# Matrix-memory heads and attention value products on full 128-row tiles, in a streaming encoder step

## The chip, the cores and the metric

The kernel runs on one core of a Trainium2 chip. The metric is device time in microseconds (us) of one execution. Beside the plain runs there is one profiled execution, from which all rows of the trace come. Engines are called as in the profile: PE is TensorE (PEld its weight loads), DVE VectorE, ACT ScalarE, POOL GpSimd, SP SyncE.

## The reference

One layer of a hybrid encoder works on 256 prompt tokens and 64 sample tokens, each with 2048 features, all in float32:

```python
z = x @ w_in                                   # 2048 x 7184
attn  = chunk_band_attention(qa, ka, va)       # 16 heads x 64, chunks of 64 queries, softmax with position bias
h_b   = mlstm(conv_silu(qk), vb, ib, fb)       # 8 heads x 128, matrix memory C, normaliser n, stabiliser m
mix   = concat(head_rms(attn), head_rms(h_b) * sigmoid(ob)) @ w_out
x1    = layer_norm(ALPHA * x + mix)
y     = layer_norm(ALPHA * x1 + (silu(x1 @ w_gate) * (x1 @ w_up)) @ w_down)   # 2048 x 5632
```

The two mixers matter here. For one matrix-memory head and one run of tokens:

```python
s   = (q @ k.T) * exp(d - m_t)                          # causal, d from the gates
num = s @ v + w_inter * (q @ C);  den = s.sum + w_inter * (q @ n)
h   = num / max(|den|, exp(-m_t))
C_new = w_old * C + (w_k * k).T @ v                     # and n_new alike
```

The prompt's 256 tokens start with an empty state, the sample's 64 tokens with a given one. In attention each chunk of 64 queries attends to the keys of up to eight chunks before it and its own, which for the sample are 512 cached keys and 64 new ones.

## The kernel before

**Projections.** All 320 tokens (256 + 64) are kept as columns; a weight matrix is cut into pieces of 128 x 1024 numbers. For every piece SP starts a load (`load_piece`, L95), ACT rounds it to a high half `hi` (L124), DVE makes the low half `lo` by subtraction (L125), and PE does three matmuls for each of the piece's eight 128 x 128 weight tiles (L174, L175, L177), 128 x 320 each: 24 matmuls per piece. `run_plan` (L151) goes through the plan of pieces. Loads run up to three pieces ahead, the split into halves two (`LOOKAHEAD`).

**What hangs on them.** When the last piece of a strip of 256 weight columns is done, the strip's function is called, and it may start generators. `advance` (L134) gives each active generator one step behind every piece, so that the steps of the mixers stand on PE between the matmuls of two pieces; a bare `yield` lets one piece go by. The strips of the input projection come in four units u, each an attention part (`A(u)`, four heads in two pairs i) and a matrix-memory part (`M(u)`, two heads); the four strips of the output gate follow. The tile framework places the instructions on the engines' queues and adds the waits; inside `tc.manual_schedule` the written order stands.

**Attention, `attn_gen` (L341).** One run per pair of heads, eight in all. It transposes values and keys to token rows (L352, L353; `vtok` holds three blocks of tokens, the third with 64 rows) and cached keys (L358), makes scores (L374 to L379), adds the bias (L386), takes exponentials (L391), transposes them into `pT` (L399, L402, and L405 for the blocks of 64 keys, which fill rows 0 to 63), and multiplies them with the values (L419): 11 terms for two heads. The weights of a value product are 64 columns of `pT`, so the two heads s = 0, 1 stand in the two column halves of the array. Seven of the 11 terms have 128 keys as array rows, four have 64.

**Matrix memory, `mlstm_gen` (L577).** One run per head, eight in all. It transposes the values (L588), weights them by the gates (L593), makes the decay matrix `E` (L595 to L597, masked on POOL by L599), the scores (L603 for the first prompt block, L604 the second, L605 the sample's 64 tokens), multiplies scores and decay (L608), transposes the keys (L614), and copies them out (L616, L617). Two pieces later eight matmuls follow in a fixed order (L624 to L631): numerators of the prompt (L624 to L626) and of the sample (L627), the sample's product with the old state (L628), and the new states (L629 to L631). Norms follow on DVE and ACT, and after three more pieces the transposes of the result (L671). Every tile of the sample has 64 token rows or columns: L605, L627, L628, L631 and the third transposes of L614, L588 and L671.

Each fp32 matmul of the mixers stands in the trace as two matmul records with a weight load each; a transpose and a matmul of the projections stand as one.

**Other things that the change touches.** `init_static` (L285) clears `qbd`, `obd` and sets the column of ones of `vt1`, on POOL. `attn_loads` (L293) starts, from POOL, the loads of cached keys and values and of the bias rows `tz` of a unit. The convolution's result `y` (L565) and `E` (L594) are tiles of rotating pools with two buffers.

Of the kernel before, what the change touches and what calls it, by code (L numbers as in the profile page):

```python
# [13 lines left out]
ALU = mybir.AluOpType  # L14
# [46 lines left out]
def _build(tc, nc, I, O, es):  # L61
# [216 lines left out]
            mixbuf[nm] = big.tile([P, 8, T], F32R, tag="Bb", bufs=2, name="mix_" + nm)  # L278


    qbd = [const.tile([P, 5, P], F32, name="qbd%d" % i) for i in range(2)]
    obd = [const.tile([P, 5, P], F32, name="obd%d" % i) for i in range(2)]
    vt1 = [const.tile([P, 3, 129], F32, name="vt%d" % i) for i in range(2)]

    def init_static():  # L285
        for t in qbd + obd:
            G.memset(t, 0.0)
        for t in vt1:
            G.memset(t[:, :, 128:129], 1.0)

    attn = {}

    def attn_loads(u):  # L293
        a = {}
        u1 = big.tile([P, 8 * T], F32, tag="Bb", bufs=2, name="u1")
# [7 lines left out]
        G.dma_start(out=a["ck"], in_=I["cache_attn_k"][:, cs].rearrange("(n p) c -> p n c", p=P))  # L303
        G.dma_start(out=a["cv"], in_=I["cache_attn_v"][:, cs].rearrange("(n p) c -> p n c", p=P))
        a["tz"] = []
        for i in range(2):
            tz = mx.tile([P, BAND], F32, tag="tz", bufs=2, name="tz")
            for s in range(2):
                h = u * 4 + i * 2 + s
                src = bass.AP(tensor=fdram.tensor, offset=fdram.offset + h * 640,  # L310
                              ap=[[1, 64], [1, BAND]])
                G.dma_start(out=tz[s * 64:(s + 1) * 64, :], in_=src)
            a["tz"].append(tz)
        a["ktok"] = mx.tile([P, 3, 256], F32, tag="ktok", bufs=1, name="ktok")
        a["vtok"] = mx.tile([P, 3, 256], F32, tag="vtok", bufs=1, name="vtok")
        a["kT"] = [None, None]
        a["vT"] = [None, None]
        attn[u] = a
# [22 lines left out]
    def attn_gen(u, i):  # L341
# [62 lines left out]
        for j, s0 in enumerate((512, 1088, 1152)):  # L404
# [2 lines left out]
        yield  # L407
        yield
        ox = w_tile()
        terms = {0: [(10, 64, vtok, 0)], 1: [(4, P, vtok, 0)],  # L410
                 2: [(7, P, vtok, 0), (9, 64, vtok, 1)], 3: [(5, P, vtok, 0), (6, P, vtok, 1)],
                 4: [(j, P, cv, j) for j in range(4)] + [(8, 64, vtok, 2)]}
        with tc.manual_schedule(engines={PE}):
            for c in range(5):
                for m, (j, n, src, k) in enumerate(terms[c]):
                    for s in range(2):
                        r = slice(s * 64, (s + 1) * 64)
                        v0 = i * P + s * 64
                        TE.matmul(ox[r, c * 64:(c + 1) * 64], pT[0:n, j, r], src[0:n, k, v0:v0 + 64],  # L419
                                  start=(m == 0), stop=(m == len(terms[c]) - 1))  # L420
        rs = mx.tile([P, 5], F32, tag="rs", bufs=2, name="rs")
        V.reciprocal(rs, sm)
# [50 lines left out]
    def gates_done(ps):  # L473
# [19 lines left out]
        st = mx.tile([P, T], F32, tag="oth", bufs=2, name="gst")  # L493
        G.memset(st, 0.0)
        g = st[0:8, :]
# [11 lines left out]
        V.tensor_scalar(st[32:40, :], wk, KSC, None, ALU.mult)  # L507
# [4 lines left out]
        V.tensor_copy(st[64:72, :], e1)  # L512
# [14 lines left out]
    def gates_gen(st):  # L527
        for _ in range(5):
            yield
        ps = w_tile()  # L530
        for i, (t0, n) in enumerate(TOK):
            TE.transpose(ps[0:n, i * P:(i + 1) * P], st[:, t0:t0 + n], ident)
        gc = const.tile([P, 3, P], F32, name="gcol")
        V.tensor_copy(gc[:, 0:2, :], ps[:, 0:256].rearrange("p (n c) -> p n c", c=P))
        V.tensor_copy(gc[0:SS, 2, :], ps[0:SS, 256:384])
# [11 lines left out]
    def qk_done(u, kind, ps):  # L547
        for i in range(2):
# [28 lines left out]
    def mlstm_gen(h, i):  # L577
# [11 lines left out]
        V.tensor_copy(vt[:, 0:2, 0:P], ps[:, 0:256].rearrange("p (n c) -> p n c", c=P))  # L589
        V.tensor_copy(vt[0:SS, 2, 0:P], ps[0:SS, 256:384])  # L590
        wkv = mx.tile([P, 3, 129], F32, tag="wkv", bufs=2, name="wkv")
        for j, (t0, n) in enumerate(TOK):
            V.tensor_scalar(wkv[0:n, j, :], vt[0:n, j, :], gc[0:n, j, 32 + h:33 + h], None, ALU.mult)  # L593
# [8 lines left out]
        ps = w_tile()  # L602
        TE.matmul(ps[:, 0:256], k[:, 0:128], q[:, 0:256], start=True, stop=True)  # L603
        TE.matmul(ps[:, 256:384], k[:, 128:256], q[:, 128:256], start=True, stop=True)  # L604
        TE.matmul(ps[0:SS, 384:448], k[:, QS0:CO], q[:, QS0:CO], start=True, stop=True)  # L605
        sT = E
        for n, c0, c1 in ((P, 0, 384), (SS, 384, 448)):
            V.scalar_tensor_tensor(out=sT[0:n, c0:c1], in0=ps[0:n, c0:c1],  # L608
                                   scalar=0.25 * 128.0 ** -0.5, in1=E[0:n, c0:c1],
                                   op0=ALU.mult, op1=ALU.mult)  # L610
        pk = w_tile()
        for j, (t0, n) in enumerate(TOK):
            t1 = QS0 if j == 2 else t0
            TE.transpose(pk[0:n, j * P:(j + 1) * P], k[:, t1:t1 + n], ident)  # L614
        kt = mx.tile([P, 3, P], F32, tag="mkt", bufs=2, name="mkt")
        S.copy(kt[:, 0:2, :], pk[:, 0:256].rearrange("p (n c) -> p n c", c=P))  # L616
        S.copy(kt[0:SS, 2, :], pk[0:SS, 256:384])  # L617
        yield
        yield
        pn = w_tile()  # L620
        pc = w_tile()
        n0, n1, n2 = pn[:, 0:129], pn[:, 129:258], pn[0:SS, 258:387]
        with tc.manual_schedule(engines={PE}):
            TE.matmul(n0, sT[:, 0:128], vt[:, 0, :], start=True, stop=True)  # L624
            TE.matmul(n1, sT[:, 128:256], vt[:, 0, :], start=True, stop=False)
            TE.matmul(n1, sT[:, 256:384], vt[:, 1, :], start=False, stop=True)  # L626
            TE.matmul(n2, sT[0:SS, 384:448], vt[0:SS, 2, :], start=True, stop=True)  # L627
            TE.matmul(pc[0:SS, 0:129], q[:, QS0:CO], cn, start=True, stop=True)  # L628
            TE.matmul(pc[:, 129:258], kt[:, 0, :], wkv[:, 0, :], start=True, stop=False)  # L629
            TE.matmul(pc[:, 129:258], kt[:, 1, :], wkv[:, 1, :], start=False, stop=True)  # L630
            TE.matmul(pc[:, 258:387], kt[0:SS, 2, :], wkv[0:SS, 2, :], start=True, stop=True)  # L631
        nd = mx.tile([P, 3, 129], F32, tag="nd", bufs=2, name="nd")
        V.tensor_copy(nd[:, 0:2, :], pn[:, 0:258].rearrange("p (n c) -> p n c", c=129))
        it = mx.tile([SS, 129], F32, tag="it", bufs=1, name="it")
        S.mul(it, pc[0:SS, 0:129], gc[0:SS, 2, 96 + h:97 + h])
        V.tensor_tensor(out=nd[0:SS, 2, :], in0=n2, in1=it, op=ALU.add)
# [30 lines left out]
        yield  # L667
        yield
        ph = w_tile()
        for j, (t0, n) in enumerate(TOK):  # L670
            TE.transpose(ph[:, t0:t0 + n], hn[0:n, j, :], ident[0:n, 0:n])  # L671
# [401 lines left out]
```

## Time and profile before

| | us |
|---|---|
| three runs | 1601.16, 1604.15, 1606.2 (median 1604.15) |
| the profiled execution | 1601.19 |
| its span, first to last instruction | 1599.2 |
| DVE busy | 836.4 (52%) |
| ACT busy | 631.9 (40%) |
| POOL busy | 122.9 (8%) |
| DMA, queue of SP | 220.23 MB, 45.2% of the 16 engines' span |

The busy time of PE is that of pipelined matmuls whose ends are modelled: a matmul of the projections shows 0.31 us, but the next one starts 0.15 us behind it. What a matmul costs is therefore read from start to start. In rows of the timeline the first column is the start of a group of like instructions that follow each other, the second its duration from the first start to the last end, then engine, line, operation, output and inputs, rows * columns of the array for PE, the moving operand, and the count. The input projection with the mixers takes the first 520 us or so, the output projection stands up to about 640 us, and the feed-forward network makes up the rest.

### The profile page before, as it was taken

What the parts mean: (1) busy time and instruction counts of PE and PEld (TensorE: products, weight loads), DVE (VectorE), ACT (ScalarE), POOL (GpSimd) and SP (SyncE); (2) the same over time, 40 slices, a digit from 0 to 9 for tenths busy, and PEclk for the clock granted to TensorE, in tenths of its full rate; (3) what the DMA queues carried; (4) which work ended last, traced back from release to release, by engine and by line L of the source; (5) the groups of instructions that cost most, each with busy time, mean ns of one, the idle gap of its engine ahead of it and who ended that gap; (6) DMA issues with size and microseconds to landing.
All of it is one profiled execution on the core that took longest, in us unless ns stands there. A gap on an engine that the chain in (4) does not pass through costs nothing.

```text
span 1599.2 us, 26591 instructions
## 1 busy us (share of the span) xinstructions
PE 1577.6 (99%) x10906; PEld 1547.5 (97%) x10906; DVE 836.4 (52%) x1512; ACT 631.9 (40%) x972; POOL 122.9 (8%) x254
## 2 busy tenths in 40 slices
PE   8999999999999999999999999999999999999997
PEld 6999999999999999899999999999999999999996
DVE  4486575665765755944334444444434434443456
ACT  4455444444444533643333233333333333323332
POOL 4013101101100100400000000000000000000004
PEclk9999999999999999999999999999999999999997
DMA  9546454554444544355444454444454444444442
GB/s 322 173 144 175 146 147 128 149 146 130 122 126 137 172 143 145 106 164 153 145 153 151 146 153 150 147 153 149 146 157 145 148 155 146 151 153 145 152 138 66
DMA packets 225545, 238.99 MB, mean 149 GB/s; under 512 B 8683, under 2 KB 219819, under 8 KB 225227
## 3 DMA queue, kind: packets, MB, share of 16 engines
q1 hardware_dynamic: 220384, 220.23, 45.2%
q0 software_dynamic: 5040, 17.07, 3.2%
q8 instruction: 85, 1.39, 0.4%
q14 instruction: 36, 0.29, 0.1%
HBM read 230.85 MB, written 10.07 MB: 151 GB/s over the span
## 4 chain that ended last, share of the span: by engine, by line
PE 95%; DVE 2%; DMA 1%; issue 0%; SPq 0%; ACT 0%; DVEq 0%; ACTq 0%
PE mm L174 30%; PE mm L177 30%; PE mm L175 29%; PE w L419 1%; DMA raw<-w_in 1%; PE w L771 1%; DVE lo L125 1%; DMA xq<-x_sample 1%; PE w L375 0%; PE w L399 0%; PE w L614 0%; DVE ytp L1035 0%; PE w L352 0%; PE w L402 0%; PE w L358 0%; PE w L377 0%
## 5 line engine op out<-in xcount | busy, mean ns | idle before, releaser
L125 DVE TENSOR_TENSOR lo<-raw,hi 128x1024 fp32r<-128x1024 f32 (+1 forms) x409 | 501.0, 1225 | 599.1 <-ACT hi L124 599.0
L124 ACT CAST hi<-raw 128x1024 fp32r<-128x1024 f32 (+1 forms) x409 | 428.1, 1047 | 746.2 <-PE mm L175 641.3
L177 PE MATMUL mm<-x1h,lo 128*128 128x320 f32 (+1 forms) x1408 | 436.5, 310 | 2.2 <-DVE lo L125 2.2
L174 PE MATMUL mm<-x1l,hi 128*128 128x320 f32 (+1 forms) x1408 | 435.5, 309 | 0.9 <-DVE np L844 0.9
L175 PE MATMUL mm<-x1h,hi 128*128 128x320 f32 (+1 forms) x1408 | 435.6, 309 | 0.0
L174 PE MATMUL mm<-xlo,hi 128*128 128x320 f32 x912 | 288.4, 316 | 0.2 <-ACT hi L124 0.2
L175 PE MATMUL mm<-xhi,hi 128*128 128x320 f32 x912 | 281.3, 309 | 0.0
L177 PE MATMUL mm<-xhi,lo 128*128 128x320 f32 x896 | 277.6, 310 | 0.5 <-DVE lo L125 0.5
L177 PEld LDWEIGHTS mm<-x1h,lo 128*128 128x128 f32 x1408 | 265.8, 189 | 2.7 <-DVE lo L125 2.7
L174 PEld LDWEIGHTS mm<-x1l,hi 128*128 128x128 f32 x1408 | 265.4, 188 | 1.4 <-DVE np L844 1.3
L175 PEld LDWEIGHTS mm<-x1h,hi 128*128 128x128 f32 x1408 | 265.4, 188 | 0.0
L174 PE MATMUL mm<-hl,hi 128*128 128x320 f32 x704 | 218.0, 310 | 0.0
L177 PE MATMUL mm<-hh,lo 128*128 128x320 f32 x704 | 217.5, 309 | 0.0
L175 PE MATMUL mm<-hh,hi 128*128 128x320 f32 x704 | 217.5, 309 | 0.0
L174 PEld LDWEIGHTS mm<-xlo,hi 128*128 128x128 f32 x912 | 171.8, 188 | 2.5 <-ACT hi L124 0.4
L175 PEld LDWEIGHTS mm<-xhi,hi 128*128 128x128 f32 x912 | 172.0, 189 | 0.0
L177 PEld LDWEIGHTS mm<-xhi,lo 128*128 128x128 f32 x896 | 168.8, 188 | 1.0 <-DVE lo L125 1.0
L175 PEld LDWEIGHTS mm<-hh,hi 128*128 128x128 f32 x704 | 132.2, 188 | 0.0
L174 PEld LDWEIGHTS mm<-hl,hi 128*128 128x128 f32 x704 | 132.2, 188 | 0.0
L177 PEld LDWEIGHTS mm<-hh,lo 128*128 128x128 f32 x704 | 132.2, 188 | 0.0
L779 POOL TENSOR_TENSOR ytp<-ytp,g 128x256 f32<-128x256 f32 x16 | 13.6, 874 | 894.6 <-ACT ytp L776 894.6
L888 DVE SCALAR_TENSOR_TENSOR y<-y,mm 128x320 f32<-128x320 f32 x96 | 46.5, 484 | 49.0 <-PE mm L177 48.6
(313 smaller groups left out, 1343.2 us busy)
## 6 DMA issues: line engine op xcount, KB each, us to landing
raw<-w_in SPq DMA_DIRECT2D x114, 512.0 KB, 3.7
raw<-w_ffn_gate SPq DMA_DIRECT2D x88, 512.0 KB, 3.5
raw<-w_ffn_up SPq DMA_DIRECT2D x88, 512.0 KB, 3.5
raw<-w_ffn_down SPq DMA_DIRECT2D x88, 512.0 KB, 3.5
raw<-w_out SPq DMA_DIRECT2D x32, 512.0 KB, 3.5
tz<-fdram POOLq DMA_DIRECT2D x16, 144.0 KB, 2.9
xq<-x_prompt SPq DMA_DIRECT2D x4, 512.0 KB, 9.1
u<-cache_attn_k POOLq DMA_DIRECT2D x4, 512.0 KB, 6.0
```

The costliest lines, as they stand in the source:

```text
L124: S.copy(hi[:, cs], raw[:, cs])
L125: V.tensor_tensor(out=lo[:, cs], in0=raw[:, cs], in1=hi[:, cs].bitcast(F32), op=ALU.subtract)
L174: TE.matmul(o, hi[:, sl], xl, start=st, stop=False)
L175: TE.matmul(o, hi[:, sl], xh, start=False, stop=en and pc.perm)
L177: TE.matmul(o, lo[:, sl], xh, start=False, stop=en)
L419: TE.matmul(ox[r, c * 64:(c + 1) * 64], pT[0:n, j, r], src[0:n, k, v0:v0 + 64], start=(m == 0), stop=(m == len(terms[c]) - 1))
L771: TE.transpose(dst[j][:, i * P:(i + 1) * P], y[:, 2 * s + i, t0:t0 + n], ident)
L779: G.tensor_tensor(out=keep[0][:, j, cs], in0=keep[0][:, j, cs], in1=late["g2"][:, cs], op=ALU.mult)
L888: V.scalar_tensor_tensor(out=y[:, c, :], in0=y[:, c, :], scalar=ALPHA if g == 0 else 1.0, in1=ps[i][:, 0:T], op0=ALU.mult, op1=ALU.add)
```

## The change

All matmuls and transposes on the sample's 64 tokens, and the value products with 64 keys, are issued with 128 rows and (outside of the value products, whose weights stay 64 columns wide) 128 weight columns. The tiles that they read get the missing rows or columns, and these are set to zero.

- `vtok`, `E` and the convolution's results become tiles that are made once (`vtok`, `Es`, `cys`), with 128 tokens' worth of space in the sample's block; `init_static` clears the space on POOL. `qbd`, `obd`, `vt1` move to the pool of the mixers.
- `attn_loads` clears rows 64 to 127 of the three 64-key blocks of `pT`, for every unit, on POOL.
- L605's weights become 128 columns of k (64 of them zero); the moving operand stays 64 columns.
- L627, L628, L631 and the transposes L532, L614, L671 take full tiles. For L627 the weights are columns 384 to 511 of `E`, for L628 128 columns of q.
- Some pairs of instructions that treated prompt and sample apart become one: the products with the decay (L608), the copies of the transposed keys (L616, L617) and of the gates (L534, L535). `wkv`, `it` and the sum of L636 are made on 128 rows.

```diff
     def init_static():
         for t in qbd + obd:
             G.memset(t, 0.0)
         for t in vt1:
+            G.memset(t[64:128, 2, :], 0.0)
             G.memset(t[:, :, 128:129], 1.0)
+        G.memset(vtok[64:128, 2, :], 0.0)
+        for i in range(2):
+            for k in "qk":
+                G.memset(cys[k][i][:, CO:CO + SS], 0.0)
+            G.memset(Es[i][:, 384:512], 0.0)
...
+    vtok = mx.tile([P, 3, 256], F32, name="vtok")
+    Es = [mx.tile([P, 512], F32, name="E%d" % i) for i in range(2)]
+    cys = {k: [mx.tile([P, CO + SS], F32, name="cy%s%d" % (k, i)) for i in range(2)] for k in "qk"}
...
-        a["vtok"] = mx.tile([P, 3, 256], F32, tag="vtok", bufs=1, name="vtok")
+        a["vtok"] = vtok
+        G.memset(a["pT"][64:128, 8:11, :], 0.0)
...
-                        TE.matmul(ox[r, c * 64:(c + 1) * 64], pT[0:n, j, r], src[0:n, k, v0:v0 + 64],
+                        TE.matmul(ox[r, c * 64:(c + 1) * 64], pT[:, j, r], src[:, k, v0:v0 + 64],
                                   start=(m == 0), stop=(m == len(terms[c]) - 1))
...
-        E = mx.tile([P, 448], F32, tag="E", bufs=2, name="E")
+        E = Es[i]
...
-        TE.matmul(ps[0:SS, 384:448], k[:, QS0:CO], q[:, QS0:CO], start=True, stop=True)
+        TE.matmul(ps[:, 384:448], k[:, QS0:QS0 + P], q[:, QS0:CO], start=True, stop=True)
         sT = E
-        for n, c0, c1 in ((P, 0, 384), (SS, 384, 448)):
-            V.scalar_tensor_tensor(out=sT[0:n, c0:c1], in0=ps[0:n, c0:c1],
-                                   scalar=0.25 * 128.0 ** -0.5, in1=E[0:n, c0:c1],
-                                   op0=ALU.mult, op1=ALU.mult)
+        V.scalar_tensor_tensor(out=sT[:, 0:448], in0=ps[:, 0:448], scalar=0.25 * 128.0 ** -0.5,
+                               in1=E[:, 0:448], op0=ALU.mult, op1=ALU.mult)
         pk = w_tile()
-        for j, (t0, n) in enumerate(TOK):
-            t1 = QS0 if j == 2 else t0
-            TE.transpose(pk[0:n, j * P:(j + 1) * P], k[:, t1:t1 + n], ident)
+        for j, t1 in enumerate((0, P, QS0)):
+            TE.transpose(pk[:, j * P:(j + 1) * P], k[:, t1:t1 + P], ident)
...
-            TE.matmul(n2, sT[0:SS, 384:448], vt[0:SS, 2, :], start=True, stop=True)
-            TE.matmul(pc[0:SS, 0:129], q[:, QS0:CO], cn, start=True, stop=True)
+            TE.matmul(n2, sT[:, 384:512], vt[:, 2, :], start=True, stop=True)
+            TE.matmul(pc[:, 0:129], q[:, QS0:QS0 + P], cn, start=True, stop=True)
...
-            TE.matmul(pc[:, 258:387], kt[0:SS, 2, :], wkv[0:SS, 2, :], start=True, stop=True)
+            TE.matmul(pc[:, 258:387], kt[:, 2, :], wkv[:, 2, :], start=True, stop=True)
...
-        for j, (t0, n) in enumerate(TOK):
-            TE.transpose(ph[:, t0:t0 + n], hn[0:n, j, :], ident[0:n, 0:n])
+        for j in range(3):
+            TE.transpose(ph[:, j * P:(j + 1) * P], hn[:, j, :], ident)
```

More of the change, by code (lines that the diff above doesn't have):

```diff
@@ L278, in mix_tiles_b @@
             mixbuf[nm] = big.tile([P, 8, T], F32R, tag="Bb", bufs=2, name="mix_" + nm)
-    qbd = [const.tile([P, 5, P], F32, name="qbd%d" % i) for i in range(2)]
-    obd = [const.tile([P, 5, P], F32, name="obd%d" % i) for i in range(2)]
-    vt1 = [const.tile([P, 3, 129], F32, name="vt%d" % i) for i in range(2)]
+    qbd = [mx.tile([P, 5, P], F32, name="qbd%d" % i) for i in range(2)]
+    obd = [mx.tile([P, 5, P], F32, name="obd%d" % i) for i in range(2)]
+    vt1 = [mx.tile([P, 3, 129], F32, name="vt%d" % i) for i in range(2)]
     def init_static():
@@ L409, in attn_gen @@
         ox = w_tile()
-        terms = {0: [(10, 64, vtok, 0)], 1: [(4, P, vtok, 0)],
-                 2: [(7, P, vtok, 0), (9, 64, vtok, 1)], 3: [(5, P, vtok, 0), (6, P, vtok, 1)],
-                 4: [(j, P, cv, j) for j in range(4)] + [(8, 64, vtok, 2)]}
+        terms = {0: [(10, vtok, 0)], 1: [(4, vtok, 0)],
+                 2: [(7, vtok, 0), (9, vtok, 1)], 3: [(5, vtok, 0), (6, vtok, 1)],
+                 4: [(j, cv, j) for j in range(4)] + [(8, vtok, 2)]}
         with tc.manual_schedule(engines={PE}):
             for c in range(5):
-                for m, (j, n, src, k) in enumerate(terms[c]):
+                for m, (j, src, k) in enumerate(terms[c]):
                     for s in range(2):
@@ L492, in gates_done @@
                                  op0=ALU.mult, op1=ALU.add)
-        st = mx.tile([P, T], F32, tag="oth", bufs=2, name="gst")
+        st = mx.tile([P, 3 * P], F32, tag="oth", bufs=2, name="gst")
         G.memset(st, 0.0)
-        g = st[0:8, :]
+        g = st[0:8, 0:T]
         V.tensor_tensor(out=g, in0=ig, in1=F, op=ALU.subtract)
@@ L506, in gates_done @@
             S.activation(wk[:, a:b], g[:, a:b], AF.Exp, bias=nM[:, b - 1:b])
-        V.tensor_scalar(st[32:40, :], wk, KSC, None, ALU.mult)
+        V.tensor_scalar(st[32:40, 0:T], wk, KSC, None, ALU.mult)
         e1 = t8("e1")
@@ L511, in gates_done @@
         S.activation(e1, e1, AF.Exp)
-        V.tensor_copy(st[64:72, :], e1)
+        V.tensor_copy(st[64:72, 0:T], e1)
         wi = mx.tile([HB, SS], F32, tag="g8_wi", name="wi")
@@ L530, in gates_gen @@
         ps = w_tile()
-        for i, (t0, n) in enumerate(TOK):
-            TE.transpose(ps[0:n, i * P:(i + 1) * P], st[:, t0:t0 + n], ident)
+        for i in range(3):
+            TE.transpose(ps[:, i * P:(i + 1) * P], st[:, i * P:(i + 1) * P], ident)
         gc = const.tile([P, 3, P], F32, name="gcol")
-        V.tensor_copy(gc[:, 0:2, :], ps[:, 0:256].rearrange("p (n c) -> p n c", c=P))
-        V.tensor_copy(gc[0:SS, 2, :], ps[0:SS, 256:384])
+        V.tensor_copy(gc, ps[:, 0:384].rearrange("p (n c) -> p n c", c=P))
         gate["col"] = gc
@@ L563, in qk_done @@
             S.activation(th, acc, AF.Tanh, scale=0.5)
-            y = mx.tile([P, CO], F32, tag="conv" + kind, bufs=2, name="cy")
-            V.scalar_tensor_tensor(out=y, in0=th, scalar=1.0, in1=acc, op0=ALU.add, op1=ALU.mult)
+            y = cys[kind][i]
+            V.scalar_tensor_tensor(out=y[:, 0:CO], in0=th, scalar=1.0, in1=acc, op0=ALU.add, op1=ALU.mult)
             ml[(kind, 2 * u + i)] = y
@@ L591, in mlstm_gen @@
         wkv = mx.tile([P, 3, 129], F32, tag="wkv", bufs=2, name="wkv")
-        for j, (t0, n) in enumerate(TOK):
-            V.tensor_scalar(wkv[0:n, j, :], vt[0:n, j, :], gc[0:n, j, 32 + h:33 + h], None, ALU.mult)
-        E = mx.tile([P, 448], F32, tag="E", bufs=2, name="E")
+        for j in range(3):
+            V.tensor_scalar(wkv[:, j, :], vt[:, j, :], gc[:, j, 32 + h:33 + h], None, ALU.mult)
+        E = Es[i]
         S.activation(E[:, 0:256], nM[:, 0:256], AF.Exp, bias=gc[:, 0, h:h + 1])
@@ L621, in mlstm_gen @@
         pc = w_tile()
-        n0, n1, n2 = pn[:, 0:129], pn[:, 129:258], pn[0:SS, 258:387]
+        n0, n1, n2 = pn[:, 0:129], pn[:, 129:258], pn[:, 258:387]
         with tc.manual_schedule(engines={PE}):
@@ L626, in mlstm_gen @@
             TE.matmul(n1, sT[:, 256:384], vt[:, 1, :], start=False, stop=True)
-            TE.matmul(n2, sT[0:SS, 384:448], vt[0:SS, 2, :], start=True, stop=True)
-            TE.matmul(pc[0:SS, 0:129], q[:, QS0:CO], cn, start=True, stop=True)
+            TE.matmul(n2, sT[:, 384:512], vt[:, 2, :], start=True, stop=True)
+            TE.matmul(pc[:, 0:129], q[:, QS0:QS0 + P], cn, start=True, stop=True)
             TE.matmul(pc[:, 129:258], kt[:, 0, :], wkv[:, 0, :], start=True, stop=False)
             TE.matmul(pc[:, 129:258], kt[:, 1, :], wkv[:, 1, :], start=False, stop=True)
-            TE.matmul(pc[:, 258:387], kt[0:SS, 2, :], wkv[0:SS, 2, :], start=True, stop=True)
+            TE.matmul(pc[:, 258:387], kt[:, 2, :], wkv[:, 2, :], start=True, stop=True)
         nd = mx.tile([P, 3, 129], F32, tag="nd", bufs=2, name="nd")
         V.tensor_copy(nd[:, 0:2, :], pn[:, 0:258].rearrange("p (n c) -> p n c", c=129))
-        it = mx.tile([SS, 129], F32, tag="it", bufs=1, name="it")
-        S.mul(it, pc[0:SS, 0:129], gc[0:SS, 2, 96 + h:97 + h])
-        V.tensor_tensor(out=nd[0:SS, 2, :], in0=n2, in1=it, op=ALU.add)
+        it = mx.tile([P, 129], F32, tag="it", bufs=1, name="it")
+        S.mul(it, pc[:, 0:129], gc[:, 2, 96 + h:97 + h])
+        V.tensor_tensor(out=nd[:, 2, :], in0=n2, in1=it, op=ALU.add)
         cw = mx.tile([P, 2, 129], F32, tag="cw", bufs=2, name="cw")
@@ L669, in mlstm_gen @@
         ph = w_tile()
-        for j, (t0, n) in enumerate(TOK):
-            TE.transpose(ph[:, t0:t0 + n], hn[0:n, j, :], ident[0:n, 0:n])
+        for j in range(3):
+            TE.transpose(ph[:, j * P:(j + 1) * P], hn[:, j, :], ident)
         ht = mx.tile([P, T], F32, tag="hst", bufs=8, name="hst")
@@ L682, in ob_done @@
                 advance()
-            th = mx.tile([P, T], F32, tag="oth", bufs=2, name="oth")
+            th = mx.tile([P, 3 * P], F32, tag="oth", bufs=2, name="oth")[:, 0:T]
             S.activation(th, ps[i][:, 0:T], AF.Tanh, scale=0.5)
```

3 lines of the change are left out of this document (1 added, 2 removed).

## The prediction

> **What bounds the kernel now.** I read the page first, then the waits of PE, the busy time by stretches, and last the timeline of PE around each edited line.
>
> ```profile
> PE 1577.6 (99%) x10906; PEld 1547.5 (97%) x10906; DVE 836.4 (52%) x1512; ACT 631.9 (40%) x972; POOL 122.9 (8%) x254
> ```
>
> ```profile
> PE 95%; DVE 2%; DMA 1%; issue 0%; SPq 0%; ACT 0%; DVEq 0%; ACTq 0%
> ```
>
> The first row is the busy time, the second the chain that ended last: 95% of it is PE. The edited lines all run between 80 and 490 us, so the question is whether PE waits for anything there. The waits of PE from 40 to 520 us have one row:
>
> ```profile
> PE mm L177 <- DVE lo L125: 0.5, 1, 0.5
> ```
>
> One wait of 0.5 us for DVE in 480 us. A busy PE is not a PE at its peak, though, and here that matters: time can go between two matmuls without any wait for another engine. The stretches (columns: length, then busy PE, PEld, DVE, ACT, POOL with counts, granted clock, DMA share, GB/s) show it:
>
> ```profile
> 80.00:120.00 40.00, 39.50 (x333) 38.11 (x332) 33.57 (x99) 22.75 (x47) 5.25 (x15) 1.00 0.50 144
> 200.00:240.00 40.00, 40.00 (x339) 38.67 (x339) 31.29 (x83) 19.15 (x37) 3.76 (x11) 1.00 0.51 148
> 640.00:680.00 40.00, 36.87 (x237) 35.71 (x235) 38.09 (x58) 27.06 (x51) 19.60 (x16) 0.96 0.34 106
> 1000.00:1200.00 200.00, 200.00 (x1365) 200.00 (x1364) 85.66 (x93) 67.83 (x77) 0.00 (x0) 1.00 0.48 150
> ```
>
> From 1000 to 1200 us PE does nothing but 128x320 matmuls: 200/1365 = 0.1465 us each, 24 of them (one piece of weights) in 3.52 us, with no idle time. That is the fastest that weights are asked for anywhere, and loads, ACT and DVE keep up. Small matmuls between pieces only stretch the time per piece, so a PE that spends less on them asks for no more than this. I conclude that PE's time from start to start is the path in the stretch of the change, and each 0.1 us taken out of it is 0.1 us of the kernel.
>
> **The eight matmuls of a head (L624 to L631).** Head 0, timeline of PE:
>
> ```profile
> 146.04 0.38 PE L624 MATMUL w<-vt,E 128*128 128x129 f32 x2
> 146.26 0.39 PE L625 MATMUL w<-vt,E 128*128 128x129 f32 x2
> 146.49 0.39 PE L626 MATMUL w<-vt,E 128*128 128x129 f32 x2
> 146.80 0.43 PE L627 MATMUL w<-vt,E 64*64 64x129 f32 x2
> 147.16 0.43 PE L628 MATMUL w<-cn,cy 128*64 128x129 f32 x2
> 147.53 0.49 PE L629 MATMUL w<-wkv,mkt 128*128 128x129 f32 x2
> 147.85 0.39 PE L630 MATMUL w<-wkv,mkt 128*128 128x129 f32 x2
> 148.17 0.49 PE L631 MATMUL w<-wkv,mkt 64*128 64x129 f32 x2
> 148.59 0.41 PE L174 MATMUL mm<-xlo,hi 128*128 128x320 f32 x1
> 148.84 0.31 PE L175 MATMUL mm<-xhi,hi 128*128 128x320 f32 x1
> ```
>
> All eight move 129 columns twice. Where the array's shape stays at 128*128 the next one starts 0.22 us on (146.04, 146.26, 146.49). Where the shape changes it takes 0.31 to 0.42: 0.31 into 64*64, 0.36 on to 128*64, 0.37 back to 128*128, 0.32 for L629 behind a change, 0.32 into 64*128, 0.42 back out. The cost hangs on the change of shape, not on the work. From L624 to the second matmul of the projection it is 148.84 - 146.04 = 2.80 us. With one shape throughout it is 8 x 0.225 = 1.80, and then one projection matmul's step, which behind a full-array group is 0.15 us (next fences: 137.75 - 137.27 = 0.48, less three transposes at 0.11). That gives 1.95; **0.85 us less per head**. The last unit shows the same spacing as the first (468.83 - 466.70 = 2.13 = 148.17 - 146.04), so I count it eight times:
>
> ```profile
> 466.70 0.38 PE L624 MATMUL w<-vt,E 128*128 128x129 f32 x2
> ```
>
> ```profile
> 468.83 0.49 PE L631 MATMUL w<-wkv,mkt 64*128 64x129 f32 x2
> ```
>
> **Scores and key transposes (L604 to L614).** The timeline of PE, head 1; the group of the value transposes L588 (last columns: busy us, mean ns of one, idle before); and two score matmuls of attention for comparison:
>
> ```profile
> 136.31 0.39 PE L604 MATMUL w<-cy 128*128 128x128 f32 x2
> 136.63 0.33 PE L605 MATMUL w<-cy 128*64 128x64 f32 x2
> 136.89 0.55 PE L614 MATMUL w<-ident,cy 128*128 128x128 f32 x3
> 137.27 0.49 PE L588 MATMUL w<-ident,mvT 128*128 128x128 f32 x3
> 137.52 0.40 PE L174 MATMUL mm<-xlo,hi 128*128 128x320 f32 x1
> 137.75 0.30 PE L175 MATMUL mm<-xhi,hi 128*128 128x320 f32 x1
> ```
>
> ```profile
> L588 PE MATMUL w<-ident,mvT 128*128 128x128 f32 x16 | 3.0, 272 | 0.0
> ```
>
> ```profile
> 78.40 0.33 PE L374 MATMUL w<-kT,qbd 128*128 128x64 f32 x2
> 78.57 0.44 PE L376 MATMUL w<-kT,qbd 128*128 128x128 f32 x2
> ```
>
> L604 to L588 takes 0.96 us now. After: L604 0.22; L605 becomes what L374 is, 128 weight columns with 64 moving ones, 0.17; three transposes at 0.11 each (L588's three last 0.49 with the last one's own 272 ns, so 0.22 for two steps), 0.33. Sum 0.72, or 0.78 if L614's slower second step (0.55 instead of 0.49) has another cause than the change of shape. I take **0.22 us less per head**, bounds 0.18 and 0.24. L588 and L614 each contain a transpose with 64 active columns and need no more for it: widening L614 and L532 is worth nothing, and costs nothing.
>
> **Transposes of the result (L671).**
>
> ```profile
> 161.91 0.58 PE L671 MATMUL w<-ident,nd 128*128 128x128 f32 x3
> 162.43 0.42 PE L174 MATMUL mm<-xlo,hi 128*128 128x320 f32 x1
> 162.68 0.31 PE L175 MATMUL mm<-xhi,hi 128*128 128x320 f32 x1
> ```
>
> The third has 64 rows. L671 to L175 is 0.77 us; L588 with its like three takes 0.48 to the same point. **0.29 us less per head**.
>
> **Value products (L419).** Second pair of unit 0, and the group of its records of one shape:
>
> ```profile
> 98.37 1.36 PE L419 MATMUL w<-vtok,u 64*64 64x64 f32 x24
> 99.56 0.64 PE L419 MATMUL w<-u,u 128*64 128x64 f32 x16
> 100.12 0.33 PE L419 MATMUL w<-vtok,u 64*64 64x64 f32 x4
> 100.38 0.41 PE L174 MATMUL mm<-xlo,hi 128*128 128x320 f32 x1
> ```
>
> ```profile
> L419 PE MATMUL w<-u,u 128*64 128x64 f32 x128 | 5.1, 222 | 0.0
> ```
>
> The first row mixes both shapes (terms of 64 and of 128 keys); the second is of one shape, and one record lasts 222 ns, so its 16 start within 0.64 - 0.22 = 0.42 us, 0.028 each. By code order the 44 records change between 64*64 and 128*64 four times. The change leaves 128*64 throughout: 44 x 0.028 = 1.23, some 0.03 for the first pair behind the entry (the four records of the third row take 0.11 where 0.08 would do), and the exit of 0.15 (100.38 less 100.23): 1.41 to 1.43 instead of 2.01. **0.59 us less per pair**. Entry and exit stay, since the weights stay 64 columns wide.
>
> **A rule that speaks against the change.** L627's 64-row passes stand behind one another like the full ones, and nothing starts beside them: L627 takes 0.36 to the next line, a full tile 0.22. The Trainium skill, TensorEngine Tiling (Array Packing), sections "Theoretical Speedup" and "When to Use Tiling", says the opposite of what the diff does: with a contraction of 64 or less one should use half the rows and so gain up to a factor of two. By the rows the whole change saves 15.6 us (sum below). By that rule it would save some 10.6 (the third rival has the mechanism and its price).
>
> **What else moves.** Per head one DVE instruction and one ACT copy go; both engines have room and PE doesn't wait for them, so nothing. On POOL the once-only clearings are nine short ones, at most 0.4 us each by the first of these rows, 2 to 3 us in all:
>
> ```profile
> 14.90 0.38 POOL L494 MEMSET gst<- 128x320 f32 x1
> ```
>
> ```profile
> 21.28 0.80 POOL L303 DMA_DIRECT2D u<-cache_attn_k  x1 [5.43 <-PE w L209]
> ```
>
> Behind them the queue idles 5.43 us for PE before the first cache load, which covers them; without that cover the first unit's loads would land 3 us later, and its scores stand behind 12 pieces of 3.52 us. The clearing of `pT` (64x384, about 0.4 us) stands in `attn_loads` behind the loads; its queue is looked at in the last rival.
>
> **Sum.** 8 x (0.85 + 0.22 + 0.29) = 10.9, and 8 x 0.59 = 4.7: 15.6 us. Against the profiled execution's 1601.19 us this gives 1585.6; against the median of three runs, which is 2.96 higher, 1588.6. The profiled one lies at the low end of a scatter of 5 us; I take the middle, **1587 us**. About 0.3% (5 us) is what a measurement of this kernel can tell from no change.
>
> **Rivals.** *DVE sets the pace.* From 80 to 120 us DVE is busy for 33.57 of 40 us, and PE's only wait, 0.5 us, falls there, right behind the value products. If DVE's queue holds the low halves back in every unit, a PE that comes earlier only waits: all that the value products save, 4.7 us, goes into that wait: 1592 us. For it: that wait, and 31.29 of 40 us from 200 to 240. Against: PE has no wait from 200 to 240, and DVE's own work there starts from PE's results, so it moves forward too.
>
> *The shape isn't the cause.* If the gaps come from changing lines, banks or operands, they stay: 1601 to 1604 us. Against: L624, L625, L626 change operands without a gap.
>
> *The narrow tiles share the array.* If 64-row passes leave the other half of the array to their neighbours, they run at half price now, and widening pays it back: L627 and L631 0.11 each, L671 0.05, and six pairs of L419 at 0.058, 0.35: 0.62 us per head and pair, 5 us in all, so 1592 us. Against: their start-to-start times. This is the page's rule from above.
>
> *Slower: the clearing of `pT` gets stuck.* POOL's queue holds bias loads that wait for DVE:
>
> ```profile
> 197.87 0.52 POOL L312 DMA_DIRECT2D tz<-fdram  x1 [6.33 <-DVE mxs L389]
> ```
>
> ```profile
> 193.29 0.58 ACT L400 COPY u<-w 128x512 f32<-128x512 f32 x1
> ```
>
> If the clearing lands behind such a load of the same unit's time and the framework makes ACT's copies into `pT` (L400, L406) wait for it, ACT, with the high halves behind it, stops from 193.29 to 198.8: 5.5 us, in four units 22 us, and each stop that cools PE costs 1.6 more (from 640 to 680 us, after PE's stall, the granted clock is 0.96 of 40 us). Without cover that is 28 us: 1615 us. Two pieces split ahead (7 us) cover a stop of 5.5, so it decides only if they are used up. Against: the clearing needs only the unit's buffer, which is free behind L419 of the unit before (100.38 us for unit 1), and the copies come at 193.29.
>
> **How the numbers follow.** Forecast 0.77; DVE 0.12; shared array 0.04; no effect 0.04; slower 0.03. The forecast's own range is 1581 (the lowest run less 15.6, and 4.5 for a wider saving or a wait that goes) to 1591 (the highest run, 1606.2, less 15.6); with the first and third rivals on a higher run it reaches 1595. Range 1581 to 1595. Faster by over 0.3%: 0.77 + 0.12 + 0.04 = 0.93; within: 0.04; slower: 0.03.
>
> **What would show it.** L624 to L631 at steps of 0.22 and all 128*128; L175 1.95 us behind L624; L605 to L614 in 0.17; L671 to L175 in 0.48; L419's 44 records in one shape, 1.4 us to the exit; PE's record counts unchanged. Wrong: gaps of 0.3 us that remain at the same lines, new rows in the waits of PE for `lo` between 80 and 490 us, or a row where ACT or PE waits for POOL.

## The result and the profile after

| | before | after |
|---|---|---|
| median | 1602.66 us (four runs, 1600.06 to 1606.2) | 1583.87 us (four runs, 1583.64 to 1585.75) |
| ratio, 95% interval | | 0.9885 [0.9873, 0.9897] |
| profiled execution | 1601.19 us | 1585.75 us |
| span | 1599.2 us | 1584.0 us |

The changed kernel is faster by 18.8 us between the medians and by 15.4 us between the profiled executions. The ratios here and below are the recorded ones; they aren't plain quotients of the medians. First the page of the changed kernel, the four longest waits of PE over the whole span, and its waits from 40 to 520 us. Line numbers are those of the changed kernel from here on: L431 is the value product (L419 before), L614 to L616 the scores (L603 to L605), L622 the key transposes (L614), L599 the value transposes (L588), L631 to L638 the eight matmuls (L624 to L631), L678 the last transposes (L671).

```profile
PE 1561.9 (99%) x10906; PEld 1543.3 (97%) x10906; DVE 834.9 (53%) x1503; ACT 631.1 (40%) x964; POOL 127.2 (8%) x267
```

```profile
PE w L209 <- DMA xq<-x_prompt: 5.5, 1, 5.5
PE w L1032 <- DVE c L1029: 5.4, 1, 5.4
PE mm L177 <- DVE lo L125: 2.7, 2, 2.2
PE mm L174 <- DVE np L851: 2.4, 1, 2.4
```

```profile
PE mm L177 <- DVE lo L125: 0.6, 1, 0.6
```

PE has the same 10906 records. In the stretch of the change it waits once, as before, for 0.6 us (0.5 before). The 2.4 us for `np` stand behind the first normalisation, long after the edited lines; it was 0.9 in the profile before, and it takes the one or the other value in different profiles of kernels that don't differ there.

The timeline of PE for the eight matmuls of head 0 and for the scores of the next head:

```profile
143.77 0.38 PE L631 MATMUL w<-vt,E 128*128 128x129 f32 x2
143.99 0.39 PE L632 MATMUL w<-vt,E 128*128 128x129 f32 x2
144.22 0.39 PE L633 MATMUL w<-vt,E 128*128 128x129 f32 x2
144.44 0.39 PE L634 MATMUL w<-vt,E 128*128 128x129 f32 x2
144.66 0.39 PE L635 MATMUL w<-cn,cyq 128*128 128x129 f32 x2
144.88 0.39 PE L636 MATMUL w<-wkv,mkt 128*128 128x129 f32 x2
145.11 0.39 PE L637 MATMUL w<-wkv,mkt 128*128 128x129 f32 x2
145.33 0.39 PE L638 MATMUL w<-wkv,mkt 128*128 128x129 f32 x2
145.47 0.39 PE L174 MATMUL mm<-xlo,hi 128*128 128x320 f32 x1
145.70 0.31 PE L175 MATMUL mm<-xhi,hi 128*128 128x320 f32 x1
```

```profile
134.50 0.39 PE L615 MATMUL w<-cyq,cyk 128*128 128x128 f32 x2
134.73 0.33 PE L616 MATMUL w<-cyq,cyk 128*128 128x64 f32 x2
134.90 0.50 PE L622 MATMUL w<-ident,cyk 128*128 128x128 f32 x3
135.23 0.49 PE L599 MATMUL w<-ident,mvT 128*128 128x128 f32 x3
135.48 0.40 PE L174 MATMUL mm<-xlo,hi 128*128 128x320 f32 x1
135.71 0.31 PE L175 MATMUL mm<-xhi,hi 128*128 128x320 f32 x1
```

Every step of the eight is 0.22 now, and L175 stands 1.93 us behind the first (2.80 before). From L615 to L599 it is 0.73 (0.96 before), L616 takes the 0.17 of its neighbour in attention, and L622's three transposes last 0.50, not 0.55: their slow second step had the change of shape for its cause. The last transposes, and the second block of value products:

```profile
157.91 0.49 PE L678 MATMUL w<-ident,nd 128*128 128x128 f32 x3
158.16 0.40 PE L174 MATMUL mm<-xlo,hi 128*128 128x320 f32 x1
158.39 0.31 PE L175 MATMUL mm<-xhi,hi 128*128 128x320 f32 x1
```

```profile
97.15 0.92 PE L431 MATMUL w<-vtok,u 128*64 128x64 f32 x24
97.90 0.64 PE L431 MATMUL w<-u,u 128*64 128x64 f32 x16
98.36 0.29 PE L431 MATMUL w<-vtok,u 128*64 128x64 f32 x4
98.58 0.41 PE L174 MATMUL mm<-xlo,hi 128*128 128x320 f32 x1
```

0.48 instead of 0.77, and 1.43 instead of 2.01. The row in the middle, whose shape was 128*64 already, is the same to the digit.

To see whether these savings reach the end I cut the time in three: up to the start of the 301st projection matmul (some 64 us, ahead of every edited matmul), from there to the first matmul of the output projection (the row of `mix_al` with its first start), and the rest. The starts are counted in the trace. Rows of the line L174 for `mix_al`, with durations min/median/max and the first and last start, of the kernel before and of the changed one:

```profile
L174 PE MATMUL mm<-mix_al,hi x128: 302/309/393, 519.1 to 629.0; 128*128 128x320 f32 x128
```

```profile
L174 PE MATMUL mm<-mix_al,hi x128: 308/309/394, 502.9 to 612.7; 128*128 128x320 f32 x128
```

| profile of | 301st projection matmul | from there to `mix_al` | runs' median |
|---|---|---|---|
| before | 65.0 | 454.1 | 1602.66 |
| before, profiled twice more | 67.3 and 64.7 | 454.1 and 454.1 | |
| pad_pool | 65.1 | 454.1 | 1602.72 |
| av_order | 67.4 | 451.8 | 1599.81 |
| av_only | 63.7 | 449.4 | 1597.35 |
| heads_only | 64.2 | 443.2 | 1589.53 |
| one_narrow | 63.8 | 441.2 | 1588.59 |
| after, and again | 64.4 and 64.4 | 438.5 and 438.5 | 1583.87, 1584.99 |
| split_again | 63.7 | 438.5 | 1585.59 |
| copy_early | 63.4 | 438.5 | 1585.19 |
| x_full, and again | 62.6 and 61.2 | 438.5 and 438.5 | 1583.09, 1581.67 |

The middle column repeats to 0.1 us for one kernel and goes from 454.1 to 438.5: 15.6 us, the forecast sum. The left column scatters by 2.6 us for one and the same kernel. The rest, from `mix_al` to the end, takes 1080.0 to 1080.1 us in ten of these profiles and 1081.2 to 1081.4 us in four (the changed kernel's first, pad_pool, av_order and one_narrow).

### The profile page after: what moved, and what is told of

Read it like the earlier page. It is cut to its first block, busy times and chain, and to the rows that moved or that the text cites. A ratio compares the mean times of both kernels' runs of the same rounds, so it can differ in the third digit from the quotient of the medians.

```text
span 1584.0 us, 26577 instructions
## 1 busy us (share of the span) xinstructions
PE 1561.9 (99%) x10906; PEld 1543.3 (97%) x10906; DVE 834.9 (53%) x1503; ACT 631.1 (40%) x964; POOL 127.2 (8%) x267
## 4 chain that ended last, share of the span: by engine, by line
PE 97%; DVE 2%; DMA 0%; issue 0%; ACT 0%; SPq 0%; DVEq 0%
PE mm L174 30%; PE mm L175 30%; PE mm L177 30%; PE w L431 1%; PE w L778 1%; PE w L387 0%; DMA raw<-w_in 0%; PE w L209 0%; DVE lo L125 0%; PE w L454 0%; PE w L411 0%; DVE ytp L1042 0%; PE w L364 0%; PE w L414 0%; PE w L370 0%; PE w L389 0%
## 5 line engine op out<-in xcount | busy, mean ns | idle before, releaser
L174 PE MATMUL mm<-x1l,hi 128*128 128x320 f32 (+1 forms) x1408 | 435.6, 309 | 2.4 <-DVE np L851 2.4
L175 PE MATMUL mm<-x1h,hi 128*128 128x320 f32 (+1 forms) x1408 | 435.5, 309 | 0.0
L174 PE MATMUL mm<-xlo,hi 128*128 128x320 f32 x912 | 287.8, 316 | 0.3 <-ACT hi L124 0.3
L175 PE MATMUL mm<-xhi,hi 128*128 128x320 f32 x912 | 281.3, 309 | 0.0
L174 PEld LDWEIGHTS mm<-x1l,hi 128*128 128x128 f32 x1408 | 265.4, 189 | 2.8 <-DVE np L851 2.7
L175 PEld LDWEIGHTS mm<-x1h,hi 128*128 128x128 f32 x1408 | 265.4, 188 | 0.0
L174 PE MATMUL mm<-hl,hi 128*128 128x320 f32 x704 | 218.0, 310 | 0.0
L175 PE MATMUL mm<-hh,hi 128*128 128x320 f32 x704 | 217.5, 309 | 0.0
L174 PEld LDWEIGHTS mm<-xlo,hi 128*128 128x128 f32 x912 | 171.8, 188 | 1.0 <-ACT hi L124 0.5
L175 PEld LDWEIGHTS mm<-xhi,hi 128*128 128x128 f32 x912 | 172.0, 189 | 0.0
L175 PEld LDWEIGHTS mm<-hh,hi 128*128 128x128 f32 x704 | 132.2, 188 | 0.0
L174 PEld LDWEIGHTS mm<-hl,hi 128*128 128x128 f32 x704 | 132.2, 188 | 0.0
```

Source lines behind the costliest of these rows:

```text
L174: TE.matmul(o, hi[:, sl], xl, start=st, stop=False)
L175: TE.matmul(o, hi[:, sl], xh, start=False, stop=en and pc.perm)
```

## The experiments

The theory: PE's time from start to start is the path, a change of the array's shape between matmuls costs 0.1 to 0.2 us whatever is computed, and the change removes these. The rivals: DVE's low halves set the pace; narrow passes cost, or gain, by themselves; the gain comes from shorter queues on the other engines.

**Value products alone (av_only).** The kernel before with only this:

```diff
+        G.memset(vtok[64:128, 2, :], 0.0)
...
+        G.memset(a["pT"][64:128, 8:11, :], 0.0)
...
-                        TE.matmul(ox[r, c * 64:(c + 1) * 64], pT[0:n, j, r], src[0:n, k, v0:v0 + 64],
+                        TE.matmul(ox[r, c * 64:(c + 1) * 64], pT[:, j, r], src[:, k, v0:v0 + 64],
```

> The kernel before with the value products alone on 128 rows (vtok made once and cleared, the 64-key blocks of pT cleared); the heads stay narrow. Theory (each change of the array's shape costs, and four of six go): a block of 44 records from its first start to the next group takes 1.43 us instead of 2.01 to 2.02, the whole 4.7 us less (ratio 0.997). Rival (DVE's low halves set the pace behind the value products): the block shrinks but the wait of PE for lo at about 117 us grows by as much, the whole within 1 us. Rival (64-row passes share the array): block at 1.75 or more, the whole 2 us less at most.

1597.35 us against 1602.74 on the same chip, ratio 0.997 [0.996, 0.9979]; a block takes 1.43 us, the middle stretch 4.7 us less. PE's wait for `lo` from 40 to 520 us:

```profile
PE mm L177 <- DVE lo L125: 0.5, 1, 0.5
```

It didn't grow. The rival in which DVE takes the gain back falls.

**Heads alone (heads_only).** The changed kernel with the 64-key terms narrow again, and without the two clearings that they need:

```diff
-                        TE.matmul(ox[r, c * 64:(c + 1) * 64], pT[:, j, r], src[:, k, v0:v0 + 64],
+                        TE.matmul(ox[r, c * 64:(c + 1) * 64], pT[0:n, j, r], src[0:n, k, v0:v0 + 64],
```

> The changed kernel with the value products put back to 64 rows for the terms of 64 keys (and without clearing vtok and pT). Theory: the heads alone are worth 8 x 1.36 = 10.9 us (ratio 0.993), and together with the value products alone they add up to the whole change, 15.6. Rival (the gain is that of one side only, or the two overlap): the two alone don't add up to the whole.

1589.53 against 1602.74, ratio 0.9919 [0.9905, 0.9932]: 13.0 us, with 10.9 at the lower end of the interval (10.9 to 15.2). The middle stretch is 10.9 us shorter; with the 4.7 of the value products that makes the 15.6 of the whole, so the two parts add up.

**Narrow, but in another order (av_order).** The kernel before; the same 44 records with the same rows, the narrow ones put together:

```diff
-                 2: [(7, P, vtok, 0), (9, 64, vtok, 1)], 3: [(5, P, vtok, 0), (6, P, vtok, 1)],
+                 2: [(9, 64, vtok, 1), (7, P, vtok, 0)], 3: [(5, P, vtok, 0), (6, P, vtok, 1)],
...
-            for c in range(5):
+            for c in (0, 2, 1, 3, 4):
```

> The kernel before; only the order of the value products' 44 records is changed, so that the terms of 64 keys stand together: the 64 rows stay narrow, the work is the same, but the shape changes twice inside a block and not four times. Theory (the change of shape costs, 0.146 us each): block 1.72 us instead of 2.01, 2.3 us less in all (ratio 0.9985). Rival (the narrow passes themselves are slow, by their operands or weight loads): block stays at 2.01, no change in time. Rival (narrow passes are fast and share the array): the four narrow pairs that now stand together start closer than 0.058 us per pair.

1599.81 against 1602.74, ratio 0.9986 [0.9977, 0.9995]. The second block in the timeline of PE:

```profile
100.47 1.06 PE L419 MATMUL w<-vtok,u 64*64 64x64 f32 x24
101.37 0.64 PE L419 MATMUL w<-u,u 128*64 128x64 f32 x16
101.93 0.33 PE L419 MATMUL w<-vtok,u 64*64 64x64 f32 x4
102.19 0.41 PE L174 MATMUL mm<-xlo,hi 128*128 128x320 f32 x1
```

Three of the 11 terms have 64 keys and eight have 128 (`terms` in the code; the description of the kernel says four and seven), so 12 of the 44 records are narrow. The first 24 records last 1.06 us instead of 1.36, the rest is as before: 1.72 us for the block, as forecast, and 2.3 us less in the middle stretch. Not one row was widened here, so it is the number of changes that costs, 0.146 us for each. The two heads' records of one pass start as a pair; the four narrow pairs that now follow one another start 58 ns apart behind the first, exactly like wide pairs: narrow passes are neither slow nor cheap. The rival in which they share the array falls with that.

**One matmul narrow again (one_narrow).** The changed kernel with

```diff
-            TE.matmul(pc[:, 0:129], q[:, QS0:QS0 + P], cn, start=True, stop=True)
+            TE.matmul(pc[0:SS, 0:129], q[:, QS0:CO], cn, start=True, stop=True)
```

and its two readers on 64 rows.

> The changed kernel with one matmul of each head narrow again: the sample's product with the old state takes 64 weight columns (and one small DVE copy more). It makes two changes of shape per head where there were none. Theory: the eight matmuls take 1.93 + 0.34 = 2.27 us to the second projection matmul (entry 203 instead of 111 ns, second pass 161 instead of 111, exit 203 instead of 111, second pass behind it 215 instead of 111), 2.7 us in all; the steps of the other six stay 0.22. Rival (each narrow matmul costs by itself, or the cost needs 64 rows): less than 0.15 us per head.

1588.59 us (ratio to before 0.9918 [0.9905, 0.9932]). The timeline:

```profile
143.25 0.38 PE L631 MATMUL w<-vt,E 128*128 128x129 f32 x2
```

```profile
143.92 0.39 PE L634 MATMUL w<-vt,E 128*128 128x129 f32 x2
144.24 0.43 PE L635 MATMUL w<-cn,cyq 128*64 128x129 f32 x2
144.60 0.49 PE L636 MATMUL w<-wkv,mkt 128*128 128x129 f32 x2
144.93 0.39 PE L637 MATMUL w<-wkv,mkt 128*128 128x129 f32 x2
145.15 0.39 PE L638 MATMUL w<-wkv,mkt 128*128 128x129 f32 x2
145.29 0.40 PE L174 MATMUL mm<-xlo,hi 128*128 128x320 f32 x1
145.53 0.31 PE L175 MATMUL mm<-xhi,hi 128*128 128x320 f32 x1
```

The steps around the narrow one are 0.32, 0.36 and 0.33, where 0.22 stood; all others stay. From the first of the eight to L175 it is 2.27 us (2.28 by the rounded rows), and the middle stretch is 2.7 us longer than in the changed kernel: 0.34 per head for two changes. All 128 rows are in use in L635, so narrow columns do it as well as narrow rows.

**Merged instructions apart again (split_again).** The changed kernel with two DVE products and two ACT copies per head, as before:

```diff
-        S.copy(kt, pk[:, 0:384].rearrange("p (n c) -> p n c", c=P))
+        S.copy(kt[:, 0:2, :], pk[:, 0:256].rearrange("p (n c) -> p n c", c=P))
+        S.copy(kt[:, 2, :], pk[:, 256:384])
```

and the product with the decay in the same manner. The copies of the gates stay merged.

> The changed kernel with the merged instructions of DVE (scores times decay) and ACT (copy of the transposed keys) made two again; PE's instructions are the same. Theory (PE alone is the path): the time of the changed kernel within 1 us, no new wait of PE. Rival (part of the gain is the engines' shorter queues): 1 to 4 us slower than the changed kernel, with a larger wait for lo or hi.

1585.59 us (1584.08 to 1588.14); the changed kernel's two medians are 1583.87 and 1584.99, its runs 1583.64 to 1587.08. By the medians alone the 0.6 to 1.7 us could be either; the trace decides. The middle stretch is 438.5 us to the digit and PE waits 0.6 us for `lo`. Merging these two pairs is worth nothing that can be measured.

**Where do 3 us more come from? (pad_pool, copy_early)** The first medians differ by more than the edited blocks give. In the trace of the changed kernel POOL issues the copy of cached keys to the output (1.8 MB) at 24.3 us, behind the first cache load, before at 15.3; and PE's wait of 1.1 us at L234 in the start was gone. My theory was that the clearings push the copy out of the way of the first weights. `pad_pool` is the kernel before with nine idle clearings; `copy_early` is the changed kernel with the copy written ahead of the loads:

```diff
+        G.memset(pad[32:64, 0:129], 0.0)
...
+    pad = mx.tile([P, 257], F32, name="pad")
```

```diff
     init_static()
+    G.dma_start(out=O["new_k_sample"][0:PAST - SS, :], in_=I["cache_attn_k"][SS:PAST, :])
     mix_tiles()
```

> The kernel before with nine idle clearings of a tile that nobody reads, as wide as those of the change, in the same place on POOL; every matmul stays as before. In POOL's order the copy of the cached keys to the output (1.8 MB, issued at 15.3 us before, at 24.3 us in the changed kernel) comes behind the first cache load, as in the changed kernel. Theory (2 to 3 us of the change's gain come from the first 33 us: the copy no longer runs while the first pieces of weights are loaded): 2 to 3 us faster than before (ratio 0.998 to 0.9985), no wait of ACT for a raw piece of over 1 us between 15 and 33 us and no wait of PE at L234, and less scatter. Rival (the copy's place doesn't matter; what the heads gained beyond 10.9 us lies elsewhere): time of before, within 1 us.

> The changed kernel, but the copy of the cached keys is written ahead of the first cache load, so that POOL issues it at about 16 us as in the kernel before; PE as in the changed kernel. Theory of the copy: 2 to 3 us slower than the changed kernel (1586 to 1587 us), with waits of ACT for raw pieces of 3 us or more in the first 33 us, more scatter. Rival: the time of the changed kernel within 1 us.

The copy moved as meant (issued at 23.8 us in the first, 16.1 us in the second), and the times did not follow: `pad_pool` 1602.72 against 1600.94, ratio 1.0005 [0.9996, 1.0014]; `copy_early` 1585.19 (0.9899 [0.9885, 0.9913]), and its start is the shortest of the kernels with narrow L209. The wait of 1.1 us at L234, too, is missing in both further profiles of the kernel before (below), so it comes and goes without the change. This theory fell.

**The changed kernel and the kernel before once more (after_again, before_look1, before_look2).**

> The changed kernel itself, again, to see what of the 18 us between the first medians belongs to the change. In all profiled executions the edited blocks give 15.6 us; 1 to 3 us more or less come from the first 30 us and from the wait at the first normalisation, which differ from execution to execution of one kernel. Theory (nothing but the edited blocks): 15 to 17 us below the kernel before on the same chip (1585 to 1587 us). Rival (the changed kernel's placing also shortens the start for good): 18 us or more again.

1584.99 against 1601.7, ratio 0.9892 [0.9874, 0.9911]: 16.7 us, within the expected 15 to 17. The interval goes from 14.3 to 20.2 us and holds the 15.6 of the edited blocks; that of the first measurement, 16.5 to 20.4 us, does not.

> The kernel before, profiled once more, for the time of its 301st projection matmul (all before any edited instruction) and of the stretches behind it. Theory (the 2 us by which the medians differ beyond 15.6 lie in the first 65 us): the 301st projection matmul at 65 us or later (65.0 before; 64.4, 64.4, 63.7 and 63.4 in profiles with wide heads and the same input code), the stretch from there to the output projection 454.1 us as before. Rival (the start is alike in both and only scatters): at 63.4 to 64.4 us.

> As the run beside it: the kernel before once more, a second sample of the start. Theory: 301st projection matmul at 65 us or later. Rival: 63.4 to 64.4 us.

The 301st projection matmul at 67.3 and 64.7 us: one bears the theory out, the other lies between the two expectations. Busy time from 0 to 66 us (length, then PE with its count and the others), of these two and of the changed kernel's second profile:

```profile
0.00:66.00 66.00, 60.49 (x352) 54.44 (x353) 26.96 (x45) 26.78 (x42) 16.83 (x44) 1.00 0.86 267
```

```profile
0.00:66.00 66.00, 59.93 (x369) 54.40 (x370) 27.57 (x46) 26.95 (x42) 16.89 (x44) 1.00 0.85 269
```

```profile
0.00:66.00 66.00, 60.00 (x371) 54.54 (x372) 27.81 (x46) 27.10 (x42) 18.71 (x54) 1.00 0.84 270
```

352, 369 and 371 matmuls have begun by 66 us. Three starts of the kernel before give 65.7 us on average, two of the changed one 64.4: 1.3 us that stand ahead of the edited matmuls. With three and two samples that scatter by 2.6 us it isn't settled whether the change shortens the start, and by what. The other runs say how much there is to explain. Taking the middle column from each median of the table leaves 1146.8 to 1148.7 us for the kernels with narrow heads (the kernel before with its four medians, 1602.66, 1602.74, 1600.94 and 1601.7) and 1145.4 to 1147.4 us for those with full heads and the old L209. The two ranges overlap, and their averages are 1.5 us apart. The first pair of medians, 1148.6 and 1145.4, comes close to the widest distance that they allow: so by these averages about half of its 3.2 us beyond the 15.6 is scatter.

**The same cure elsewhere (x_full).** The changed kernel, with the input transposes on 128 rows:

```diff
+        G.memset(t[64:128, 2, :], 0.0)
         nc.sync.dma_start(out=t[0:SS, 2, :], in_=xs[:, q * 512:(q + 1) * 512])
...
-                TE.transpose(ps[:, t0:t0 + n], xq[q][0:n, i, kk * P:(kk + 1) * P], ident[0:n, 0:n])
+                TE.transpose(ps[:, i * P:(i + 1) * P], xq[q][:, i, kk * P:(kk + 1) * P], ident)
```

> The changed kernel with the same cure for the 16 transposes of the input's 64 sample rows in the first 30 us (L209, still 64 rows; their tiles cleared on POOL first). Each of them now makes two changes of shape: 203 + 203 ns where 109 + 109 would do, 0.19 us, 3.0 us in all. Theory (PE's time is the path wherever PE isn't waiting): those behind the first four (12 of 16) are on the path, 2 us faster than the changed kernel. Rival (the first 30 us go at the pace of the loads, and PE only waits more): no change, with larger waits of ACT for raw pieces or of PE for the input.

> The changed kernel with the 16 transposes of L209 on 128 rows too, beside the changed kernel in one call. Theory: 1 to 2 us faster than the changed kernel, since its first 300 projection matmuls were done at 62.6 us instead of 64.4 and 63.4 in two profiles of kernels with narrow ones. Rival (the start follows the loads): within 1 us of the changed kernel.

1583.09 (0.9881 [0.9866, 0.9896]), and in the second measurement 1581.67 (0.9871 [0.9849, 0.9892]) beside 1584.99 for the changed kernel. Over both measurements the eight runs have a median of 1582.4 us (1580.99 to 1583.49), the changed kernel's eight 1584.6 (1583.64 to 1587.08). Twelve transposes, in the changed kernel and in this one, where the line is L210:

```profile
19.38 2.30 PE L209 MATMUL w<-ident,xq 128*128 128x128 f32 x12
21.60 0.42 PE L174 MATMUL mm<-xlo,hi 128*128 128x320 f32 x1
```

```profile
18.54 1.47 PE L210 MATMUL w<-ident,xq 128*128 128x128 f32 x12
19.77 0.39 PE L175 MATMUL mm<-xlo,hi 128*128 128x320 f32 x1
```

From the first transpose to the next matmul it is 1.23 us instead of 2.22, 1.0 us less for this group, and the same for the next one at 25.23 us: 2.0 us. That is 0.25 us for each narrow transpose, where the expectation had 0.19: it left out that the second step behind a change is slow too (165 ns instead of 109). The group at 5.5 us gives nothing, and the one at 13.1 us takes 2.33 us instead of 2.65 in the first profile of this kernel and 1.23 in its second. This is the fastest version of all: 2.2 us below the changed kernel by these medians, 3.3 us in the measurement that has both.

## Why the prediction was right

- *PE from start to start is the path.* Right. The middle stretch fell by 15.6 us, and the only wait of PE in it is 0.6 us.
- *The eight matmuls.* 1.93 us from the first to L175, where the working had 1.95; 0.86 per head.
- *Scores and key transposes.* 0.73, where the working had 0.72 or 0.78; the lower one, since the slow second step went too.
- *Last transposes.* 0.48 forecast and measured.
- *Value products.* 1.43, the upper end of 1.41 to 1.43. Four changes inside the block at the 0.146 us of av_order are 0.58 us, the whole of what was saved.
- *What else moves.* The merged products and key copies are worth nothing, by split_again. The nine clearings took 0.15 to 0.35 us each; the first cache load is issued at 21.97 us instead of 21.28, and no wait of PE comes of it; that POOL's order changes behind them (bias loads first, the copy of keys later) I had not foreseen, and by pad_pool and copy_early it didn't matter.
- *The sum against the median.* This is the term that was off, by 3.1 us of 1587. The spans of the profiled executions differ by 15.2 us: 15.6 in the blocks and 0.7 from the start, less 1.2 behind `mix_al` (1080.0 us to the end before, 1081.2 after). That 1.2 is not the longer wait for `np`, which ends 153.4 to 153.5 us behind the start of `mix_al` in every profile. Behind it the granted clock differs, 0.86 in the first profile of the changed kernel and 1.00 in the second, whose rest takes 1080.1 us (length, PE, clock, DMA share, GB/s):

```profile
657.90:662.90 5.00, 5.00 (x32) 0.86 0.54 175
```

```profile
657.90:662.90 5.00, 5.00 (x36) 1.00 0.51 167
```

  The medians differ by 18.8, and by 16.7 in the second measurement. I took 1587 us, midway between the profiled execution less the sum and the median less the sum; the median came at 1583.87, and at 1584.99 the second time. That the first medians lie 3.2 us further apart than the sum is in good part luck, as told above; whether the remaining 1.5 us or so belong to the change is open.
- *Rivals.* DVE (0.12): PE's wait for `lo` went from 0.5 to 0.6 us. In the kernel before it stands at 117.80 us, 17 us behind the value products; the working took it to stand right behind them. Narrow passes that share the array: the spacing in av_order speaks against it. No effect, and `pT`'s clearing stuck: neither seen; POOL clears `pT` at 23.33, 101.67, 212.81 and 318.13 us, over 50 us ahead of ACT's first copy into it each time (77.62, 188.76, 294.09 and 399.41), and nothing waits for it.

The Trainium skill, TensorEngine Tiling (Array Packing), "Key Properties", says that a change of tiling mode drains the engine, a change of tile within a mode not. The runs agree that a change of shape costs time and put a price on it: 0.146 us per change in the value products, 0.34 for the two around one narrow matmul; that it is a drain no run shows. In one case no cost shows. The third transpose of L599 has 64 columns and stands as 128*64 in the trace, a change of shape by the trace, and yet L175 starts 0.48 us behind the first of L599's three transposes, just as it does behind L678's three full ones. L599's third transposes by themselves:

```profile
L599 PE MATMUL w<-ident,mvT 128*64 128x128 f32 x8 | 2.2, 273 | 0.0
```

The rule of the Trainium skill, same page, "When to Use Tiling", that a contraction of 64 rows calls for row tiling by two, holds no gain here: the kernel issues no second matmul for the other 64 rows. A version that packs two narrow tiles was not run.

## What to carry to other kernels

Look at starts, not at busy time: PE showed 99%, and one wait of 0.5 us in the stretch of the change, and 15.6 us lay between its matmuls there. Where matmuls of different row or column counts alternate, put like shapes together or fill up the small ones with zeros; the zeros cost nothing that shows in the steps (0.22 us for a tile half of zeros as for a full one), a change of shape costs 0.1 to 0.2 us each way. Transposes that are narrow in columns alone can stay as they are. When the edit is smaller than the scatter of the start, compare a stretch between two fixed instructions, which repeats to 0.1 us, and not only the medians.

## What the runs showed of the hardware that I had not expected

- The stretch of 450 us behind the start repeats to 0.1 us between profiles (454.1 three times, 438.5 in six profiles of four kernels), while the first 65 us scatter by 2.6 us. The rest takes 1080.0 to 1080.1 us or 1081.2 to 1081.4: in the four longer profiles the granted clock was 0.82 to 0.86 in the 5 us behind the first normalisation, in the ten others 1.00. All but a few tenths of a microsecond of the scatter between the profiles of one kernel comes from these two places.
- A transpose with 64 active columns (the third of L588 or L599) stands as 128*64 in the trace and costs nothing extra; one with 64 rows (L671's and L209's third) costs 0.29 us in a group of three with the step behind it, and 0.25 us each in L209's row of twelve. So the shape alone doesn't decide: L605 and L635, matmuls with 128*64, do pay.
- The place of a transfer in POOL's order is sensitive: nine clearings of 0.15 to 0.30 us each moved a copy of 1.8 MB from 15.3 to 23.8 us.
